# Where sixteen steps of weight sums stand in a fused encoder block, which queue carries them, and which engine does some small evacuations

## The chip, the cores and the metric

One core of one Trainium2 chip runs the whole program; its engines are TensorE (PE: matmuls, and PEld its weight loads), VectorE (DVE), ScalarE (ACT), GpSimd (POOL) and SyncE (SP, which here only issues DMAs). The metric is the device time of one execution in microseconds (us), lower is better; a kernel's time is the median of its runs.

## The reference

One layer of a streaming encoder on x of 256 tokens by 1024, in float32. Each stage adds its normalised result to x:

```python
x += 0.5 * rms_post(swiglu(rms_pre(x)))            # ffn 1, width 2816
h  = rms_pre(x); q_a, f_a, i_a, g_a, q_b, k_b, v_b, f_b, gates = split(h @ w_in)
f  = lb + (1 - lb) * sigmoid(f_a); k = 1 - f; q = silu(q_a)
o_t = S_t^T q_t,  S_t = diag(f_t) S_{t-1} + k_t i_t^T       # recurrence, 8 heads of 128
A  = rms(o) * silu(g_a)
B  = softmax(q_b k_b^T / sqrt(128) + decay of f_b, causal) v_b   # "FoX"
y  = sigmoid(gate_A) * (A @ w_branch_a) + sigmoid(gate_B) * (B @ w_branch_b)
x += rms_post(y @ w_out)
x += rms_post(cross_attention(rms_pre(x), rms(mem)))  # the memory stage, 4 heads
x += 0.5 * rms_post(swiglu(rms_pre(x)))            # ffn 2
```

## The kernel before

The kernel is one program for one core, written for a scheduler that keeps each engine's order close to the order of the text; `issue_after(x)` puts an instruction behind x in that order, and `after(i)` does so for the i-th matmul of a log, with priority. Nothing loops at run time.

**Weights.** Every weight passes through TensorE as two float32r parts. `load_split` (L129) loads 512 KB, [128, 1024], by SP's queue into one of 4 `raw` buffers; ScalarE casts it to `hi` (L137) and VectorE takes the rest, `lo = raw - hi` (L138), each into one of 8 buffers. A projection does three matmuls per block: hi by hi, hi by lo, lo by hi (`proj_tok` L177, `proj_col` L186); four units of weights make a chunk of 512 columns. An instruction on SP's queue that waits holds all that stand behind it.

**Order of the stages.** ffn 1; then the mixer's projections i_a, f_a, q_a (L779 to L836), the recurrence with gf (g_a and f_b's eight columns together, in three chunks of 344), k_b and q_b (L935 to L996), FoX's scores, v_b and the gates (L1032 to L1127), the branches and w_out, the memory stage (mk, mq, mv, the attention, mo, L1205 to L1305), ffn 2.

**The recurrence** is done by levels, m = 0, 1, 2, ..., 32, 64, 128, for two groups of four heads: `products(m)` multiplies k and q tiles on TensorE, `grow(m)` multiplies halves of q and k by the decay products on VectorE (L898, L903, L904, and the next products at L908), `keep` stores the products. The products of one level need the growth of the level before. They are put among the projection matmuls of gf, k_b and q_b by counts in the log, `R_AT` (L45); the scheduler places the growth and the splits of the weights on VectorE in between.

**The sums.** ffn 2 multiplies by a Strassen-like scheme in four "quads", and this needs sums of its weights. They are made early, in 16 steps, `steps` (L745): `load_step` (L749) brings 2 x 512 KB into one of two `wide` slots, `at` (L762) makes four VectorE adds of 128x512 on it (L771 to L774) and stores 2 x 512 KB to DRAM (L776), then calls for the next load. `SUMS_AT` (L56) names the places where the steps stand: `(name, c)` is the c-th evacuation of that projection. Only the first two loads go by SP's queue; the other loads and all stores by GpSimd's queue. Loads after the fourth wait for the gates' bias rows, which use a `wide` buffer (L1112).

**Evacuations.** f is scaled and shifted by VectorE (L821, eight of 128x256) and k = 1 - f too (L823). q is silu(z): ScalarE's Sigmoid (L834), then VectorE's product (L835). g_a likewise: Sigmoid (L946), then one VectorE instruction that scales and multiplies (L947, six of them). FoX's softmax is scaled by VectorE (L1057).

**The tail.** `post_last` (L346) ends the second token half: the squares' sums on ScalarE, a square root there (L357), two small Newton steps on VectorE (L364 to L368), then the last scaling of 1024 columns: 256 by ScalarE and GpSimd (L373, L374), 512 and 256 by VectorE (L376), three stores by two queues. `act_evac` (L409) issues a small Sqrt to a scratch tile (L417) after a Silu of the last quad, so that ScalarE's table is loaded.

Of the kernel before, what the change touches and what calls it, by code (L numbers as in the profile page):

```python
# [16 lines left out]
P = 128  # L17
D = 1024
T = 256
# [59 lines left out]
def block_kernel(ctx: ExitStack, tc: tile.TileContext, wts, head_in, gf_in, x_in, mem_in, memT_in, cols, rows, fbias, masks, out):  # L79
# [42 lines left out]

    cache = {}
    loads = []

    def parts_of():
        return [wp.tile([P, D], F32R, tag=t, name=nm(t), bufs=8) for t in ("hi", "lo")]

    def load_split(src, n=512):  # L129

        raw = wp.tile([P, D], F32, tag="raw", name=nm("raw"), bufs=4)
        hi, lo = parts_of()
        r, h, l = raw, hi, lo
        if n < 512:
            r, h, l = (p.rearrange("p (k n) -> p k n", k=2)[:, :, :n] for p in (raw, hi, lo))
        loads.append(nc.sync.dma_start(r, src).ins)
        S.copy(h, r)  # L137
        V.tensor_tensor(out=l, in0=r, in1=h.bitcast(F32), op=ALU.subtract)  # L138
        return hi, lo

    def unit(name, i):
# [204 lines left out]
    def post_last(ps, h, grow, factor):  # L346

        s = s1(2, name="ss2")
        ts = []
        for j in range(2):  # L350
            ssq(s[:, j : j + 1], ps[j])
            if j == 0:
                sums = s1(name="v")
                V.tensor_scalar(out=sums, in0=s[:, 0:1], scalar1=D * EPS, scalar2=None, op0=ALU.add)
            else:
                y = s1(name="y")
                S.activation(y, s[:, 1:2], AF.Sqrt, bias=sums)  # L357
                v = s1(name="v")
                V.tensor_tensor(out=v, in0=s[:, 1:2], in1=sums, op=ALU.add)
            t = sp.tile([P, 512], F32, tag="z2", name=nm("post"), bufs=3)  # L360
            V.scalar_tensor_tensor(out=t, in0=ps[j], scalar=-factor * 16.0, in1=grow[:, j * 512 : (j + 1) * 512], op0=ALU.mult, op1=ALU.mult)
            ts.append(t)
        z = s1(name="y")
        V.reciprocal(z, y)  # L364
        t = s1(name="t")
        V.scalar_tensor_tensor(out=t, in0=v, scalar=z, in1=z, op0=ALU.mult, op1=ALU.mult)
        r = s1(name="y")
        V.scalar_tensor_tensor(out=r, in0=t, scalar=3.0, in1=z, op0=ALU.subtract, op1=ALU.mult)  # L368
        for eng, a, b, queue in ((G, 512, 768, nc.scalar), (V, 0, 512, nc.sync), (V, 768, 1024, nc.sync)):
            xh = xs[:, h, a:b]  # L370
            t = ts[a // 512][:, a % 512 : a % 512 + b - a]
            if eng is G:
                S.activation(t, t, AF.Copy, scale=r)  # L373
                G.tensor_tensor(out=xh, in0=t, in1=xh, op=ALU.add)  # L374
            else:
                V.scalar_tensor_tensor(out=xh, in0=t, scalar=r, in1=xh, op0=ALU.mult, op1=ALU.add)  # L376
            queue.dma_start(out[h * P : (h + 1) * P, a:b], xh)


    def ffn(w_in, w_dn, X, r2, n_tok, i_row, quads, sums, first_half, second_half=None):  # L380
# [366 lines left out]
    brows = []  # L747

    def load_step():  # L749
        if len(slots) < len(steps) and (brows or len(slots) < TO_GATES):  # L750
            c, q, i = steps[len(slots)]
            W = wp.tile([P, 2, 2, 512], F32, tag="wide", name=nm("wide"), bufs=2)
            for e in range(2):
                part, src = W[:, e].rearrange("p j n -> p (j n)"), wts[_AT["f2_in"] + 4 * (c + e - 1) + 2 * q + i]
                if len(slots) < 2:
                    with tc.issue_after(loads[-1]):
                        nc.sync.dma_start(part, src)
                else:
                    G.dma_start(part, src)
            slots.append(W)  # L760

    def at(name, c=0):  # L762

        if (name, c) not in SUMS_AT:
            return
        k = SUMS_AT.index((name, c))
        (u, q, i), W = steps[k], slots[k]
        last = next(x for x in reversed(nc.cur_bb.bb.instructions) if x.engine == mybir.EngineType.DVE)
        t1, t4, t3, t2 = (W[:, a, b] for a in range(2) for b in range(2))
        with tc.issue_after(last):  # L770
            V.tensor_tensor(out=t1, in0=t1, in1=t3, op=ALU.add)  # L771
            V.tensor_tensor(out=t3, in0=t3, in1=t2, op=ALU.add)
            V.tensor_tensor(out=t2, in0=t1, in1=t2, op=ALU.add)  # L773
            V.tensor_tensor(out=t4, in0=t2, in1=t4, op=ALU.add)  # L774
        for e in range(2):
# [35 lines left out]
    for c in range(2):  # L811
        u = chunk("f_a", c)
        f, k = m4([P, 4, T], n="f"), m4([P, 4, T], n="k")
        for j in range(2):
# [8 lines left out]
        V.tensor_scalar(out=k, in0=f, scalar1=-1.0, scalar2=1.0, op0=ALU.mult, op1=ALU.add)  # L823
        fT.append(f)
        kT_.append(k)
    for c in range(2):
        u = chunk("q_a", c)
        q = m4([P, 4, T], n="q")
        for j in range(2):
            js = slice(2 * j, 2 * j + 2)  # L830
            ps = proj_col2(X2, u, (2 * j, 2 * j + 1))
            z = sp.tile([P, 2, T], F32, tag="z2", name=nm("z2"), bufs=3)
            V.tensor_tensor(out=z, in0=ps, in1=bc(row2, [P, 2, T], 1), op=ALU.mult)
            S.activation(q[:, js], z, AF.Sigmoid)  # L834
            V.tensor_tensor(out=q[:, js], in0=q[:, js], in1=z, op=ALU.mult)  # L835
        qT_.append(q)  # L836


# [100 lines left out]
    for c in range(3):  # L939
        u = [load_split(gf_in[4 * c + i], GF) for i in range(4)]  # L940
        n = min(GF, D - c * GF)
        for h in range(2):
            ps = mm()
            proj_tok(ps[:, :GF], X2, u, h, GF)
            sg = sp.tile([P, 512], F32, tag="z2", name=nm("z2"), bufs=3)[:, :n]
            sig_last = S.activation(sg, ps[:, :n], AF.Sigmoid, scale=r2[h]).ins  # L946
            V.scalar_tensor_tensor(out=Gt[h][:, c * GF : c * GF + n], in0=ps[:, :n], scalar=r2[h], in1=sg, op0=ALU.mult, op1=ALU.mult)  # L947
            if n < GF:
                V.tensor_scalar(out=zf[h], in0=ps[:, n:GF], scalar1=r2[h], scalar2=None, op0=ALU.mult)


    fz = sp.tile([8, T], F32, tag="fz", name="fz", bufs=1)
# [20 lines left out]
    for c in range(2):  # L973
        for name, lst, sc in (("k_b", kb_, 1.0), ("q_b", qb_, 1.0 / math.sqrt(128.0))):
# [3 lines left out]
            for j in range(2):  # L978
                ps = proj_col2(X2, u, (2 * j, 2 * j + 1))
                for i in range(2):  # L980
                    V.scalar_tensor_tensor(out=t[:, 2 * j + i], in0=ps[:, i], scalar=sc, in1=row2, op0=ALU.mult, op1=ALU.mult)
            lst.append(t)
            if c == 0 and name == "k_b":
                forget(m + 30)
# [47 lines left out]
    def fox_scores(g):  # L1032
        k, q = kb_[g], qb_[g]
        for h in range(2):
# [22 lines left out]
            V.tensor_tensor(out=p, in0=p, in1=bc(sm, [P, 4, ns], 2), op=ALU.mult)  # L1057
            ps_[g, h] = p

    def fox_pT(g):  # L1060
# [32 lines left out]
    for c in range(2):  # L1093
        u = chunk("v_b", c)
        t = m4([P, 2, 512], n="v_b")
        for h in range(2):
            ps = mm()
            proj_tok(ps, X2, u, h)
            S.activation(t[:, h, :], ps, AF.Copy, scale=r2[h])
        vb_.append(t)  # L1100
    for h in range(2):
        with after(len(log) - L_OA * (2 - h)):
# [5 lines left out]
    def gates(c):  # L1108
        u = chunk("gates", c)
        z = m4([P, 2, 512], n="zg")  # L1110
        if c == 0:
            brows.append(wp.tile([P, 4, 512], F32, tag="wide", name=nm("brow"), bufs=2))  # L1112
        brow = brows[0][:, c]
# [8 lines left out]

    m = len(log)
    gates(0)
    load_step()
    for g in range(2):
        with after(m + F_T[g]):  # L1127
            fox_pT(g)
# [3 lines left out]

    memT_s = [m4([P, 4, T], n="memT") for _ in range(2)]
    for j in range(2):
        nc.sync.dma_start(memT_s[j], memT_in[:, 4 * j : 4 * j + 4, :])
    M = Pair()
    for kb in range(KB):
        gain_split(M, kb, memT_s[kb // 4][:, kb % 4, :], G_KV)
    rm = []
    for h in range(2):  # L1140
        ms = m4([P, D], n="ms")
        nc.sync.dma_start(ms, mem_in[:, h])
# [6 lines left out]
    load_step()  # L1149
    g2 = load_row(1)  # L1150
    Y = Pair()

# [244 lines left out]
```

## Time and profile before

| | us |
|---|---|
| three runs, median (lowest to highest) | 785.71 (785.20 to 786.02) |
| the profiled execution | 785.17 |
| its span in the profile | 783.4 |
| TensorE busy | 774.3 |
| VectorE busy | 646.2 |
| ScalarE busy | 468.4 |

The profile is one execution; what lies around its span is 1.77 us. Instructions are named by engine, line of the kernel, operation and tiles (out<-in). In a listing the first column is the start in us from the span's start and the second the duration; brackets say how long the engine stood idle before and what released it. Instructions that follow one another on VectorE overlap a little in the records, so their cost is read from start to start.

### The profile page before, as it was taken

The page shows a single profiled execution, that of the slowest core. Times are in us where ns is not written, and L with a number is a line of the kernel's source. Part 1 is how long each engine was busy: PE and PEld are TensorE (multiplying, and loading weights), DVE is VectorE, ACT ScalarE, POOL GpSimd, SP SyncE. Part 2 cuts the span into 40 slices and gives each one's busy share as a digit, 9 for nine tenths or more (in the row PEclk, how much of TensorE's full clock was granted, in tenths as well). Part 3 has the DMA queues.
Part 4 walks back from the last instruction along what each step waited for, and adds up shares of the span by engine and source line. Part 5 has one row for each costly group of instructions (what it writes and reads, how often), then busy time and mean ns, then how long its engine had stood idle before and what let it go on. Part 6 is the DMA issues. An engine that isn't in the chain of part 4 may idle for free.

```text
span 783.4 us, 13175 instructions
## 1 busy us (share of the span) xinstructions
PE 774.3 (99%) x5004; PEld 669.9 (86%) x5004; DVE 646.2 (82%) x1004; ACT 468.4 (60%) x704; POOL 48.4 (6%) x81
## 2 busy tenths in 40 slices
PE   9999999999999999999999999999999999999996
PEld 7888888888899999998888888999888888888884
DVE  7889989968798898578777886998787889888864
ACT  7665664756752447347674444744646758677763
POOL 0000000000121100200001221011110000000000
PEclk9999999999999999999999999999999999999999
DMA  9794484476687655753479999579875279899831
GB/s 349 249 327 154 155 309 161 147 233 245 251 305 257 183 191 164 232 212 121 152 278 341 377 338 378 203 275 375 319 226 185 83 261 388 311 314 323 339 122 54
DMA packets 57392, 193.61 MB, mean 247 GB/s; under 512 B 6249, under 2 KB 9713, under 8 KB 57329
## 3 DMA queue, kind: packets, MB, share of 16 engines
q1 hardware_dynamic: 48080, 159.60, 57.9%
q0 software_dynamic: 9104, 33.04, 12.1%
q8 instruction: 39, 0.64, 0.3%
q14 instruction: 25, 0.20, 0.1%
q10 hardware_dynamic: 144, 0.13, 0.0%
HBM read 174.92 MB, written 17.83 MB: 246 GB/s over the span
## 4 chain that ended last, share of the span: by engine, by line
PE 99%; ACT 0%; DVE 0%; issue 0%; DVEq 0%; ACTq 0%
PE mm L93 64%; PE acc L93 28%; PE tr L93 4%; PE tr L395 1%; PE tr L315 1%; PE tr L1067 0%; PE tr L1158 0%; PE tr L1264 0%; ACT L357 0%; PE tr L406 0%; DVEq L1393 0%; DVE xs L376 0%; ACT hT L156 0%; ACT y L357 0%; ACT junk L243 0%
## 5 line engine op out<-in xcount | busy, mean ns | idle before, releaser
L138 DVE TENSOR_TENSOR lo<-raw,hi 128x1024 fp32r<-128x1024 f32 (+1 forms) x228 | 271.3, 1205 | 53.0 <-ACT hi L137 49.2
L137 ACT CAST hi<-raw 128x1024 fp32r<-128x1024 f32 (+1 forms) x228 | 232.1, 1036 | 118.2 <-PE mm L93 69.5
L93 PE MATMUL mm<-lo,hT 128*128 128x512 f32 (+1 forms) x448 | 171.2, 386 | 0.0
L93 PE MATMUL mm<-hi,hT 128*128 128x512 f32 (+1 forms) x448 | 170.7, 385 | 0.0
L93 PE MATMUL mm<-hi,lT 128*128 128x512 f32 (+1 forms) x448 | 170.4, 384 | 0.0
L93 PE MATMUL acc<-hi,act 128*128 128x512 f32 x352 | 113.2, 391 | 0.0
L93 PE MATMUL mm<-hT,hi 128*128 128x256 f32 x384 | 109.0, 284 | 0.1
L93 PE MATMUL mm<-hT,lo 128*128 128x256 f32 x384 | 109.0, 284 | 0.0
L93 PE MATMUL mm<-lT,hi 128*128 128x256 f32 x384 | 108.9, 284 | 0.0
L93 PEld LDWEIGHTS mm<-hi,hT 128*128 128x128 f32 x448 | 84.1, 188 | 16.1 <-ACT hT L271 0.7
L93 PEld LDWEIGHTS mm<-hi,lT 128*128 128x128 f32 x448 | 84.1, 188 | 15.8 <-DVE lT L272 0.5
L93 PEld LDWEIGHTS mm<-lo,hT 128*128 128x128 f32 x448 | 84.0, 188 | 15.0 <-DVE lo L138 0.4
L93 PEld LDWEIGHTS acc<-hi,act 128*128 128x128 f32 x352 | 65.9, 188 | 13.7 <-DVE act L157 0.2
L93 PEld LDWEIGHTS mm<-hT,hi 128*128 128x128 f32 x384 | 73.6, 192 | 0.5 <-issue 0.3
L93 PEld LDWEIGHTS mm<-lT,hi 128*128 128x128 f32 x384 | 73.6, 192 | 0.1
L93 PEld LDWEIGHTS mm<-hT,lo 128*128 128x128 f32 x384 | 73.6, 192 | 0.1
L93 PE MATMUL acc<-lo,act 128*128 128x512 f32 x176 | 69.0, 392 | 0.0
L157 DVE TENSOR_TENSOR lo<-wide,hi 128x1024 fp32r<-128x1024 f32 x40 | 47.9, 1219 | 1.5 <-ACT hi L156 1.1
L156 ACT CAST hi<-wide 128x1024 fp32r<-128x1024 f32 x40 | 41.5, 1052 | 11.5 <-DVE wide L494 7.5
L776 POOL DMA_DIRECT2D sums<-wide x32 | 23.6, 738 | 357.8 <-DVE wide L773 240.8
L93 PEld LDWEIGHTS acc<-lo,act 128*128 128x128 f32 x176 | 33.1, 188 | 6.7
L93 PE MATMUL mm<-hi,sh 128*128 128x512 f32 x96 | 37.5, 390 | 0.0
(243 smaller groups left out, 1126.8 us busy)
## 6 DMA issues: line engine op xcount, KB each, us to landing
raw<-in_wts_dram SPq DMA_DIRECT2D x232, 512.0 KB, 5.1
sums<-wide POOLq DMA_DIRECT2D x32, 512.0 KB, 6.2
wide<-sums SPq DMA_DIRECT2D x32, 512.0 KB, 6.9
wide<-in_wts_dram POOLq DMA_DIRECT2D x28, 512.0 KB, 6.7
wide<-in_wts_dram SPq DMA_DIRECT2D x12, 512.0 KB, 6.4
raw<-in_gf_dram SPq DMA_DIRECT2D x12, 344.0 KB, 4.9
head<-in_head_dram SPq DMA_DIRECT2D x8, 388.0 KB, 5.7
grow<-in_rows_dram SPq DMA_DIRECT2D x4, 512.0 KB, 8.9
```

The costliest lines, as they stand in the source:

```text
L93: log.append(PE.matmul(*args, **kw).ins)
L137: S.copy(h, r)
L138: V.tensor_tensor(out=l, in0=r, in1=h.bitcast(F32), op=ALU.subtract)
L156: S.copy(hi, src)
L157: V.tensor_tensor(out=lo, in0=src, in1=hi.bitcast(F32), op=ALU.subtract)
L315: PE.transpose(ps[:, j * P : (j + 1) * P], src(kb), ident)
L395: PE.transpose(trv[:, j, h * P : (h + 1) * P], ats[c, h][:, j * P : (j + 1) * P], ident)
L776: G.dma_start(sums[u][2 * e : 2 * e + 2, q, :, i * 512 : i * 512 + 512].rearrange("k p n -> p k n"), W[:, e])
```

## The change

- `SUMS_AT`: ten steps now stand among the projections from i_a to q_b (before, four), six behind the gates and in the branches as before, none in the memory stage.
- All loads and stores of the sums go by SP's queue. A store is called for when 8 more weight loads have been written (`TO_STORE`), the next load 4 weight loads after that (`TO_LOAD`); both are put behind the newest weight load. New are `later` and `tick`, which keep this list.
- ScalarE scales and shifts f, makes k, and scales FoX's softmax (four instructions where VectorE had one). q and g_a become ScalarE's Silu directly, without VectorE's product; the first Silu stands behind k.
- The gates' bias rows lie in `z2` tiles of 128x512 and come, like memory's inputs, by GpSimd's queue.
- `post_last` scales 2 x 512 columns on VectorE and stores by SP's queue; the warm-up Sqrt stands behind the last Silu of ffn 2.

Because the scheduler fits the rest around this, other instructions move as well. The matmuls are the same 5004. In the changed program 18 projection matmuls stand between the level-32 and the level-64 products, 46 before; and the split of the fourth unit of the first q_b chunk stands behind the growth of level 32 and one add, where it stood ahead of that growth.

```diff
-SUMS_AT = (
-    ("i_a", 1), ("f_a", 0), ("f_a", 2), ("f_a", 3), ("gates", 1), ("gates", 3), ("br_a", 0), ("br_b", 0),
-    ("br_a", 1), ("br_b", 1), ("mk", 1), ("mk", 3), ("mq", 0), ("mq", 1), ("mv", 1), ("ao", 0),
-)
-TO_GATES = 4
+SUMS_AT = (("i_a", 1), ("f_a", 1), ("f_a", 3), ("q_a",1), ("q_a",3), ("gf",1), ("gf",3), ("gf",5), ("k_b", 1), ("q_b", 1), ("gates", 1), ("gates", 3), ("br_a", 0), ("br_b", 0), ("br_a", 1), ("br_b", 1),)
+TO_STORE = 8
+TO_LOAD = 4
...
+    due = []
+
+    def later(n, f):
+        due.append((len(loads) + n, f))
+
+    def tick():
+        while due and due[0][0] <= len(loads):
+            due.pop(0)[1]()
...
         V.tensor_tensor(out=l, in0=r, in1=h.bitcast(F32), op=ALU.subtract)
+        tick()
         return hi, lo
...
-        for eng, a, b, queue in ((G, 512, 768, nc.scalar), (V, 0, 512, nc.sync), (V, 768, 1024, nc.sync)):
...
+        for j, (t, xh) in enumerate(zip(ts, x_halves(h))):
+            V.scalar_tensor_tensor(out=xh, in0=t, scalar=r, in1=xh, op0=ALU.mult, op1=ALU.add)
+            nc.sync.dma_start(out[h * P : (h + 1) * P, j * 512 : (j + 1) * 512], xh)
...
-            if c == NFF - 1 and (c, 1 - h) in ats and not first_half:
+            if len(ats) == 2 * NFF - 1 and not first_half:
...
-                if len(slots) < 2:
-                    with tc.issue_after(loads[-1]):
-                        nc.sync.dma_start(part, src)
-                else:
-                    G.dma_start(part, src)
...
+        for e in range(2):
+            with tc.issue_after(loads[-1]):
+                nc.sync.dma_start(W[:, e].rearrange("p j n -> p (j n)"), wts[_AT["f2_in"] + 4 * (c + e - 1) + 2 * q + i])
...
         k = SUMS_AT.index((name, c))
+        while len(slots) <= k:
+            due.pop(0)[1]()
...
-        for e in range(2):
-            G.dma_start(sums[u][2 * e : 2 * e + 2, q, :, i * 512 : i * 512 + 512].rearrange("k p n -> p k n"), W[:, e])
-        load_step()
+
+        def store():
+            for e in range(2):
+                with tc.issue_after(loads[-1]):
+                    nc.sync.dma_start(sums[u][2 * e : 2 * e + 2, q, :, i * 512 : i * 512 + 512].rearrange("k p n -> p k n"), W[:, e])
+            later(TO_LOAD, load_step)
+
+        later(TO_STORE, store)
...
-                V.tensor_scalar(out=f[:, i], in0=f[:, i], scalar1=olb[:, hd : hd + 1], scalar2=lbv[:, hd : hd + 1], op0=ALU.mult, op1=ALU.add)
+                S.activation(f[:, i], f[:, i], AF.Identity, bias=lbv[:, hd : hd + 1], scale=olb[:, hd : hd + 1])
...
-            S.activation(q[:, js], z, AF.Sigmoid)
-            V.tensor_tensor(out=q[:, js], in0=q[:, js], in1=z, op=ALU.mult)
+            V.tensor_tensor(out=q[:, js], in0=ps, in1=bc(row2, [P, 2, T], 1), op=ALU.mult)
+            with tc.issue_after(k_last):
+                S.activation(q[:, js], q[:, js], AF.Silu)
+            at("q_a", 2 * c + j)
...
-            sig_last = S.activation(sg, ps[:, :n], AF.Sigmoid, scale=r2[h]).ins
-            V.scalar_tensor_tensor(out=Gt[h][:, c * GF : c * GF + n], in0=ps[:, :n], scalar=r2[h], in1=sg, op0=ALU.mult, op1=ALU.mult)
+            sig_last = S.activation(Gt[h][:, c * GF : c * GF + n], ps[:, :n], AF.Silu, scale=r2[h]).ins
...
-            V.tensor_tensor(out=p, in0=p, in1=bc(sm, [P, 4, ns], 2), op=ALU.mult)
+            for i in range(4):
+                S.activation(p[:, i], p[:, i], AF.Copy, scale=sm[:, i : i + 1])
...
-        with tc.issue_after(loads[-1]):
-            nc.sync.dma_start(brow, rows[4 + c // 2, c % 2 * 512 : c % 2 * 512 + 512].partition_broadcast(P))
+        brow = sp.tile([P, 512], F32, tag="z2", name=nm("brow"), bufs=3)
+        G.dma_start(brow, rows[4 + c // 2, c % 2 * 512 : c % 2 * 512 + 512].partition_broadcast(P))
```

More of the change, by code (lines that the diff above doesn't have):

```diff
@@ L368, in post_last @@
         V.scalar_tensor_tensor(out=r, in0=t, scalar=3.0, in1=z, op0=ALU.subtract, op1=ALU.mult)
-        for eng, a, b, queue in ((G, 512, 768, nc.scalar), (V, 0, 512, nc.sync), (V, 768, 1024, nc.sync)):
[L370 to L374, printed above, removed]
-            else:
-                V.scalar_tensor_tensor(out=xh, in0=t, scalar=r, in1=xh, op0=ALU.mult, op1=ALU.add)
-            queue.dma_start(out[h * P : (h + 1) * P, a:b], xh)
+        for j, (t, xh) in enumerate(zip(ts, x_halves(h))):
+            V.scalar_tensor_tensor(out=xh, in0=t, scalar=r, in1=xh, op0=ALU.mult, op1=ALU.add)
+            nc.sync.dma_start(out[h * P : (h + 1) * P, j * 512 : (j + 1) * 512], xh)
     def ffn(w_in, w_dn, X, r2, n_tok, i_row, quads, sums, first_half, second_half=None):
@@ L746, in block_kernel @@
     slots = []
-    brows = []
     def load_step():
-        if len(slots) < len(steps) and (brows or len(slots) < TO_GATES):
-            c, q, i = steps[len(slots)]
-            W = wp.tile([P, 2, 2, 512], F32, tag="wide", name=nm("wide"), bufs=2)
-            for e in range(2):
-                part, src = W[:, e].rearrange("p j n -> p (j n)"), wts[_AT["f2_in"] + 4 * (c + e - 1) + 2 * q + i]
-                if len(slots) < 2:
-                    with tc.issue_after(loads[-1]):
-                        nc.sync.dma_start(part, src)
-                else:
-                    G.dma_start(part, src)
-            slots.append(W)
+        if len(slots) == len(steps):
+            return
+        c, q, i = steps[len(slots)]
+        W = wp.tile([P, 2, 2, 512], F32, tag="wide", name=nm("wide"), bufs=2)
+        for e in range(2):
+            with tc.issue_after(loads[-1]):
+                nc.sync.dma_start(W[:, e].rearrange("p j n -> p (j n)"), wts[_AT["f2_in"] + 4 * (c + e - 1) + 2 * q + i])
+        slots.append(W)
     def at(name, c=0):
@@ L774, in at @@
             V.tensor_tensor(out=t4, in0=t2, in1=t4, op=ALU.add)
-        for e in range(2):
-            G.dma_start(sums[u][2 * e : 2 * e + 2, q, :, i * 512 : i * 512 + 512].rearrange("k p n -> p k n"), W[:, e])
-        load_step()
+        def store():
[4 more added lines that the diff above has]
+        later(TO_STORE, store)
     iv = [m4([P, 2, 512], n="iv") for _ in range(2)]
@@ L820, in block_kernel @@
                 hd = 4 * c + i
-                V.tensor_scalar(out=f[:, i], in0=f[:, i], scalar1=olb[:, hd : hd + 1], scalar2=lbv[:, hd : hd + 1], op0=ALU.mult, op1=ALU.add)
+                S.activation(f[:, i], f[:, i], AF.Identity, bias=lbv[:, hd : hd + 1], scale=olb[:, hd : hd + 1])
             at("f_a", 2 * c + j)
-        V.tensor_scalar(out=k, in0=f, scalar1=-1.0, scalar2=1.0, op0=ALU.mult, op1=ALU.add)
+        k_last = S.activation(k, f, AF.Copy, bias=1.0, scale=-1.0).ins
         fT.append(f)
@@ L831, in block_kernel @@
             ps = proj_col2(X2, u, (2 * j, 2 * j + 1))
-            z = sp.tile([P, 2, T], F32, tag="z2", name=nm("z2"), bufs=3)
-            V.tensor_tensor(out=z, in0=ps, in1=bc(row2, [P, 2, T], 1), op=ALU.mult)
-            S.activation(q[:, js], z, AF.Sigmoid)
-            V.tensor_tensor(out=q[:, js], in0=q[:, js], in1=z, op=ALU.mult)
+            V.tensor_tensor(out=q[:, js], in0=ps, in1=bc(row2, [P, 2, T], 1), op=ALU.mult)
+            with tc.issue_after(k_last):
+                S.activation(q[:, js], q[:, js], AF.Silu)
+            at("q_a", 2 * c + j)
         qT_.append(q)
@@ L944, in block_kernel @@
             proj_tok(ps[:, :GF], X2, u, h, GF)
-            sg = sp.tile([P, 512], F32, tag="z2", name=nm("z2"), bufs=3)[:, :n]
-            sig_last = S.activation(sg, ps[:, :n], AF.Sigmoid, scale=r2[h]).ins
-            V.scalar_tensor_tensor(out=Gt[h][:, c * GF : c * GF + n], in0=ps[:, :n], scalar=r2[h], in1=sg, op0=ALU.mult, op1=ALU.mult)
+            sig_last = S.activation(Gt[h][:, c * GF : c * GF + n], ps[:, :n], AF.Silu, scale=r2[h]).ins
             if n < GF:
                 V.tensor_scalar(out=zf[h], in0=ps[:, n:GF], scalar1=r2[h], scalar2=None, op0=ALU.mult)
+            at("gf", 2 * c + h)
     fz = sp.tile([8, T], F32, tag="fz", name="fz", bufs=1)
@@ L981, in block_kernel @@
                     V.scalar_tensor_tensor(out=t[:, 2 * j + i], in0=ps[:, i], scalar=sc, in1=row2, op0=ALU.mult, op1=ALU.mult)
+                at(name, 2 * c + j)
             lst.append(t)
@@ L1099, in block_kernel @@
             S.activation(t[:, h, :], ps, AF.Copy, scale=r2[h])
+            at("v_b", 2 * c + h)
         vb_.append(t)
@@ L1110, in gates @@
         z = m4([P, 2, 512], n="zg")
-        if c == 0:
-            brows.append(wp.tile([P, 4, 512], F32, tag="wide", name=nm("brow"), bufs=2))
-        brow = brows[0][:, c]
-        with tc.issue_after(loads[-1]):
-            nc.sync.dma_start(brow, rows[4 + c // 2, c % 2 * 512 : c % 2 * 512 + 512].partition_broadcast(P))
+        brow = sp.tile([P, 512], F32, tag="z2", name=nm("brow"), bufs=3)
+        G.dma_start(brow, rows[4 + c // 2, c % 2 * 512 : c % 2 * 512 + 512].partition_broadcast(P))
         for h in range(2):
@@ L1134, in block_kernel @@
     for j in range(2):
-        nc.sync.dma_start(memT_s[j], memT_in[:, 4 * j : 4 * j + 4, :])
+        G.dma_start(memT_s[j], memT_in[:, 4 * j : 4 * j + 4, :])
     M = Pair()
@@ L1141, in block_kernel @@
         ms = m4([P, D], n="ms")
-        nc.sync.dma_start(ms, mem_in[:, h])
+        G.dma_start(ms, mem_in[:, h])
         rm.append(rstd_x([ms[:, 0:512], ms[:, 512:]]))
```

2 lines of the change are left out of this document (removed).

## The prediction

> **What bounds the kernel now.** I read the page's busy times and the chain of work that ended last first, then the waits of TensorE.
>
> ```profile
> span 783.4 us, 13175 instructions
> PE 774.3 (99%) x5004; PEld 669.9 (86%) x5004; DVE 646.2 (82%) x1004; ACT 468.4 (60%) x704; POOL 48.4 (6%) x81
> PE 99%; ACT 0%; DVE 0%; issue 0%; DVEq 0%; ACTq 0%
> ```
>
> ```profile
> PE tr L93 <- DVE ones L206: 1.1, 1, 1.1
> ```
>
> The chain is TensorE from end to end, and its list of waits has one row: 1.1 us, once, at the start. So no work taken off another engine and no transfer made cheaper can shorten the middle. The change can gain only behind the last matmul, and it loses wherever TensorE is now made to wait. The question is how much room the engines beside it have. Busy time by stage answers that (us, then PE, PEld, DVE, ACT and POOL busy, TensorE's clock, DMA share, GB/s):
>
> ```profile
> 205.00:256.30 51.30, 51.30 (x412) 50.51 (x411) 41.34 (x61) 25.71 (x33) 7.19 (x12) 1.00 0.83 294
> 256.30:306.40 50.10, 50.05 (x1119) 48.15 (x1119) 45.03 (x81) 27.19 (x40) 3.74 (x8) 1.00 0.59 181
> 480.00:620.00 140.00, 139.88 (x868) 125.19 (x868) 116.12 (x221) 82.69 (x150) 14.40 (x23) 1.00 0.72 256
> ```
>
> The second row is the stretch in which the recurrence's level products stand between the gf, k_b and q_b projections: VectorE is busy 45.0 of 50.1 us, so it has 5.1 us of room. The third row is the memory stage: TensorE is short of 0.12 us in 140. What is freed there can be worth next to nothing; I put it at 0, at most 0.5 us over the whole run.
>
> **The change, part by part.**
>
> *The tail.* These rows are the end of the run (start, duration; the matmul is the last one), with the stores' landing times from the page's list of DMA issues.
>
> ```profile
> 775.29 0.39 PE L93 MATMUL acc<-hi,act 128*128 128x512 f32 x1
> ...
> 776.27 0.19 ACT L243 ACTIVATION_READ_ACCUMULATOR junk<-acc 128x1 f32 x1
> 776.49 1.28 ACT L357 ACT_TABLE_LOAD   x1
> 776.50 0.69 DVE L361 SCALAR_TENSOR_TENSOR post<-acc,grow 128x512 f32<-128x512 f32 x1 [1.24 <-ACT junk L243]
> 777.11 0.15 DVE L359 TENSOR_TENSOR v<-ss,v 128x1 f32<-128x1 f32 x1
> 777.78 0.29 ACT L357 ACTIVATE y<-ss,v 128x1 f32<-128x1 f32 x1
> 778.11 0.17 DVE L364 RECIPROCAL y<-y 128x1 f32<-128x1 f32 x1 [0.85 <-ACT y L357]
> ...
> 778.76 1.61 DVE L376 SCALAR_TENSOR_TENSOR xs<-post,y,xs 128x512 f32<-128x512 f32 x2
> ...
> 779.54 1.19 SPq L377 DMA_DIRECT2D out_dram<-xs  x2
> ```
>
> ```profile
> out_dram<-xs SPq DMA_DIRECT2D x3, 256.0 KB, 2.0
> ...
> out_dram<-xs SPq DMA_DIRECT2D x1, 128.0 KB, 1.9
> ```
>
> The square root at 777.78 stands behind a table load of 1.28 us, and VectorE waits 0.85 us for it. The load is there because the warm-up of Sqrt is issued behind a Silu that is not the last one, and Silu's table came back. The change issues it behind the really last Silu, well ahead of the tail. Then the root runs at 776.49 and ends before 776.8; next late is VectorE itself, which is through its product and sum at 777.11 + 0.15 = 777.26. The reciprocal starts at about 777.28 in place of 778.11: 0.83 us sooner. Behind it the old tail has two VectorE passes (1.61 us, a 512-wide one and, as the code has it, a 256-wide one, the listing grouping them) and GpSimd's quarter; the new one has two 512-wide passes of 0.60 start to start. From 778.76 − 0.83 = 777.93 these end at 777.93 + 0.60 + 0.69 = 779.2 in place of 780.37, and the last transfer, now 256 KB, takes 2.0 in place of 1.9. Bounds 0.7 (a semaphore's hop more) to 1.1; I take **−0.9 us**.
>
> *VectorE's work in the stretch 256.3 to 306.4.* The levels form a chain: products on TensorE, growth of q and k on VectorE, next products. Durations come from these two views, a listing of VectorE just ahead of the level-64 products, and the stretch's groups (busy, mean ns):
>
> ```profile
> 302.87 1.23 DVE L138 TENSOR_TENSOR lo<-raw,hi 128x1024 fp32r<-128x1024 f32 x1 [1.89 <-ACT hi L137]
> 304.01 0.68 DVE L903 TENSOR_TENSOR q<-q,aux 128x512 f32<-128x512 f32 x1
> 304.61 0.68 DVE L904 TENSOR_TENSOR k<-k,aux 128x512 f32<-128x512 f32 x1
> 305.21 0.68 DVE L903 TENSOR_TENSOR q<-q,aux 128x512 f32<-128x512 f32 x1
> 305.82 0.68 DVE L904 TENSOR_TENSOR k<-k,aux 128x512 f32<-128x512 f32 x1
> ```
>
> ```profile
> L138 DVE TENSOR_TENSOR lo<-raw,hi 128x688 fp32r<-128x688 f32 x7 | 6.1, 872 | 0.2
> ...
> L898 DVE TENSOR_TENSOR q<-q,f 128x1024 f32<-128x1024 f32 x2 | 2.4, 1221 | 0.7 <-PE acc L93 0.7
> L947 DVE SCALAR_TENSOR_TENSOR G<-mm,rstd,z 128x344 f32<-128x344 f32 x4 | 2.3, 565 | 0.6 <-ACT z L946 0.6
> ...
> L835 DVE TENSOR_TENSOR q<-q,z 128x512 f32<-128x512 f32 x1 | 0.7, 691 | 0.0
> ```
>
> ```profile
> L773 DVE TENSOR_TENSOR wide<-wide 128x512 f32<-128x512 f32 x16 | 11.0, 688 | 0.3
> ```
>
> Start to start, a 512-wide add costs 0.60, a 1024-wide split or product 1.14, a 688-wide split 0.79 us; rows overlap by some 0.08. From the last q evacuation (TensorE sets its time, 256.31) to the end of the level-32 growth, the changed program's order on VectorE differs so: six products into G leave for ScalarE's Silu (6 × 0.49 = −2.9); one q product leaves (−0.6); three 1024-wide splits, ten before and seven now, stand behind the growth (−3.4); eighteen adds of sums come in (those of q_a 3, gf 1, gf 3, gf 5 and the first two of k_b 1; 18 × 0.60 = +10.8). Before, that work took 45.1 us and ended at 306.5. Now it is 45.1 − 2.9 − 0.6 − 3.4 + 10.8 = 49.0 us, and would end at 305.3 if VectorE never idled.
>
> *When TensorE wants it.* The products stand elsewhere too:
>
> ```profile
> 301.24 1.21 PE L93 MATMUL acc<-q,k 128*32 128x32 f32 x64
> 302.37 0.39 PE L93 MATMUL mm<-lT,hi 128*128 128x256 f32 x1
> 302.59 0.28 PE L93 MATMUL mm<-hT,lo 128*128 128x256 f32 x1
> 302.71 0.28 PE L93 MATMUL mm<-hT,hi 128*128 128x256 f32 x1
> 302.83 0.29 PE L93 MATMUL mm<-lT,hi 128*128 128x256 f32 x1
> ...
> 308.08 1.09 PE L93 MATMUL acc<-q,k 128*64 128x64 f32 x30
> ```
>
> Between the level-32 and the level-64 products stand 46 projection matmuls of 0.12 us; in the changed order 18. So TensorE comes to the level-64 products not at 308.08 but at about 302.37 + 18 × 0.12 + 0.15 = 304.7, and to the second recurrence's half of them 0.55 us later, 305.25. The old growth ended 1.6 us ahead of 308.08; the new one, at best 305.3, has no room. Behind these products TensorE has 5 more matmuls (0.6 us), then wants the split of the fourth q_b unit, which VectorE does after the growth and one more add: 0.60 + 1.14 = 1.74 against 0.55 + 0.6 = 1.15, so another 0.6 us. Without any idle time on VectorE the stall is 0.05 + 0.6 = 0.65 us; each us of idle adds one.
>
> *The transfers.* Stores and loads of sums move from GpSimd's queue to SP's, where the weights are issued in order. Landing times (min, median, max) at two places of the trace, first of three weight loads behind four wide halves on SP, then of four weight loads while the same kind of stores went out by GpSimd:
>
> ```profile
> 184.31 1.94 SPq L757 DMA_DIRECT2D wide<-in_wts_dram  x4
> 186.35 2.28 SPq L136 DMA_DIRECT2D raw<-in_wts_dram  x3
> ```
>
> ```profile
> DMA to landing us min/median/max: 8.7/9.0/9.3
> ```
>
> ```profile
> DMA to landing us min/median/max: 4.6/5.3/5.5
> ```
>
> ```profile
> wide<-in_wts_dram SPq DMA_DIRECT2D x12, 512.0 KB, 6.4
> ```
>
> A store on SP waits for VectorE's fourth add, a load for the landing of the store before it in its slot, and all weight loads behind stand still meanwhile. In the changed order gf 3's two wide halves stand between and behind gf 1's two stores, and behind them the third k_b unit's load. Ahead of the end of gf 1's adds VectorE has the evacuation, eight adds, four small splits, two 1024-wide products, four growths and some 1.3 us of masks: 0.6 + 4.8 + 3.2 + 2.3 + 2.4 + 1.3 = 14.6, so they end near 271; four issues of 0.43 each later the second load half is out, near 272.8, and it lands 6.4 later, at 279.2. VectorE has two small and two large splits, four growths and 0.8 of masks before gf 3's first add (1.6 + 2.3 + 2.4 + 0.8 = 7.1) and reaches it at 278.0: 1.2 us idle. The k_b load is issued near 272, behind four halves, lands after 8.7, and ScalarE's cast takes 1 us more: 281.9 against 280.7, another 1.2. That is 2.4 us; with 5.3 us for either landing both are in time and it is 0; with 9.3 for both it is about 4. I take 2.4, from the row of the same queue and position. The growth then ends at 305.3 + 2.4 = 307.7 and TensorE's stall is 2.45 + 0.6 = **+3.0 us** (0.65 to 4.8).
>
> A rule speaks against this. The Trainium skill, page "DMA: Bandwidth & Descriptors", section "Issuing engines are not separate DMA queues", says that transfers started by different engines run on the same 16 DMA engines and that only issue time depends on who starts them. By it the landing would be GpSimd's and the stall 0.65; the two landing rows here differ, but so does what else is in flight at the two places, so they do not refute it.
>
> *The other stages.* ScalarE takes 8 scalings of f, two of 1−f, and 16 scalings in FoX's softmax; it was busy 25.7 of 51.3 and about half elsewhere, and TensorE waited for none of it. VectorE loses these:
>
> ```profile
> L1057 DVE TENSOR_TENSOR p<-p,sm 128x512 f32<-128x512 f32 (+1 forms) x4 | 3.8, 949 | 0.0
> ```
>
> The scalings, four in a row per tile where VectorE made one pass of 0.95, stand ahead of the transposes, which stand some matmuls later in the new order. I take 0; bounds −0.5 and, about one such pass too late, +1. Fewer sums in the memory stage (6 × 2.4 us of VectorE): 0. The gate rows on GpSimd's queue: 0, since the weights that follow land sooner without them.
>
> **The sum**, against the profiled execution's 785.17 (span 783.4 and 1.77 around it): 785.17 − 0.9 + 3.0 = 787.3. The median of the three runs, 785.71, lies 0.54 above it: **787.8**.
>
> **The rivals.** *The queue does not matter (the other side).* If SP's in-order issue delays nothing that lands, VectorE idles only as TensorE lets it, the level-64 stall is 0.65 us or less, and the tail decides: 785.71 − 0.9 + 0.65 = 785.5, with up to 0.65 and 0.5 of the memory stage more in its favour, 784.3. For it: 5.3 us landings beside GpSimd's stores, a DMA share of 0.59 in the stretch. Against: the 8.7 to 9.3 row. It decides from landings of under some 6 us. Range 784.0 to 786.4. This is also the result by the skill's rule.
>
> *SP's queue closes in on itself.* Five steps end in the 50.1 us of the stretch, so those on one slot are 20 us apart; adds of 2.4, a store and a load of 9 each make 20.4, and some wait at the queue's head. If each of gf 3, gf 5, k_b 1 and q_b 1 comes 1.5 us late, idle is 6, the stall 6.05 + 0.6, and the time 785.71 − 0.9 + 6.65 = 791.5 (789.3 to 793). For it: every store now blocks weight loads. Against: the same trips took 5 to 7 us on GpSimd's queue.
>
> *FoX or the gates stall as well*: the forecast plus 1 us, 788.8.
>
> **How the numbers follow.** The forecast (its own range 786.4 to 789.2) 0.42; the queue does not matter 0.27; SP closes in 0.20; FoX as well 0.11. Below 784.7 and above 791.2 I leave some 0.2. About 0.2% or 1.57 us is what a measurement of this kernel tells from no change: slower starts at 787.28, faster at 784.14. The forecast's range lies two thirds beyond 787.28 (0.28), with 0.20 and 0.11: slower 0.59. Same: 0.14 of the forecast and 0.21 of the second case, 0.35. Faster: its lowest end, 0.06.
>
> **What would show it.** Right: the table load gone from the tail and the reciprocal near 0.8 us sooner after the last matmul; a TensorE wait of 2 to 3 us at the level-64 products for VectorE's q or k, then a smaller one for a lo; VectorE idle ahead of gf 3's first add, released by a DMA; the memory stage the same length with less VectorE and DMA. Wrong: no TensorE wait between 256 and 312 (second case), waits at several levels or weight loads landing after 10 us (third), waits after 345 (fourth).

## The result and the profile after

| | us |
|---|---|
| before, median of 6 runs in this comparison | 785.19 |
| changed, median of 6 runs (lowest to highest) | 794.23 (790.42 to 799.28) |
| ratio, 95% interval | 1.0116 (1.0093 to 1.0139) |
| the profiled execution of the changed kernel, its span | 796.39, 794.6 |

The change makes the kernel 9.0 us slower, where 2.1 was forecast and 791.2 was the upper end of the range. It also makes the time unsteady: six runs spread over 9 us, those of the kernel before over 1.1.

The page's first line and its chain, then TensorE's waits (engine, line and tile <- who released it: us in total, times, longest):

```profile
span 794.6 us, 13118 instructions
...
PE 75%; DVE 10%; DMA 9%; issue 3%; ACT 2%; SPq 1%; DVEq 0%; ACTq 0%
```

```profile
PE mm L91 <- DVE zf L951: 2.6, 1, 2.6
PE tr L91 <- DVE ct L1032: 2.0, 1, 2.0
PE acc L91 <- ACT q L838: 1.2, 1, 1.2
PE tr L322 <- DVE lT L279: 1.1, 1, 1.1
PE tr L91 <- DVE ones L213: 1.1, 1, 1.1
PE acc L91 <- ACT hT L278: 0.6, 1, 0.6
```

The chain, which was TensorE alone, now runs through VectorE, ScalarE and the transfers. No line of the list is the wait that was forecast, at the level-64 products for q or k. The stages, in the columns of the table shown before:

```profile
205.00:256.30 51.30, 51.30 (x408) 50.36 (x407) 35.78 (x48) 32.77 (x42) 0.00 (x0) 1.00 0.88 293
256.30:306.40 50.10, 46.24 (x1021) 44.29 (x1020) 45.00 (x82) 22.41 (x31) 2.27 (x6) 0.97 0.97 334
306.40:345.00 38.60, 38.60 (x399) 38.16 (x398) 28.85 (x42) 17.59 (x26) 5.88 (x7) 1.00 0.92 337
480.00:620.00 140.00, 138.76 (x859) 124.39 (x858) 101.42 (x184) 80.15 (x138) 0.00 (x0) 1.00 0.57 187
```

VectorE's load in the second row is what it was, 45.0 us. What changed is the last two columns: the DMA share there rose from 0.59 to 0.97 and what was moved from 181 to 334 GB/s. In the memory stage both fell, and TensorE gained nothing there, as forecast; it lost 1.1 us, the wait for `lT` (L279) in the list. How a late transfer reaches TensorE is read from the chain in order of time (start, duration):

```profile
275.28 7.81 DMA raw<-in_wts_dram
...
283.17 1.05 ACT hi L143
...
284.25 1.23 DVE lo L144
285.47 0.60 DVE wide L772
286.07 0.60 DVE q L907
...
289.15 0.60 DVE wide L773
289.75 0.15 DVE zf L951
289.90 0.04 issue
289.94 3.42 PE mm L91 x17
```

A weight load takes 7.8 us to land. ScalarE's cast waits for it, VectorE's split waits for the cast, and behind the split, in VectorE's order, stand an add, the growth of q and k, the last add and the small evacuation `zf` (L951), which alone keeps a PSUM buffer from TensorE. TensorE stands still for 2.6 us. And then it is slow:

```profile
286.00:289.90 3.90, 1.30 (x9) 1.01 (x7) 3.90 (x12) 1.52 (x2) 0.00 (x0) 1.00 1.00 344
289.90:293.30 3.40, 3.36 (x19) 3.14 (x19) 3.05 (x4) 2.06 (x3) 0.00 (x0) 0.61 0.93 324
...
353.90:358.70 4.80, 4.65 (x17) 3.82 (x18) 4.73 (x21) 0.96 (x4) 0.00 (x0) 0.67 0.56 218
```

The granted clock is 0.61 in the 3.4 us behind the stall and 0.67 in the 4.8 us behind the next (2.0 us, in FoX): 3.4 × 0.39 + 4.8 × 0.33 = 2.9 us more. With the five new waits, 2.6 + 2.0 + 1.2 + 1.1 + 0.6 = 7.5, this is 10.4 of the 12.0 us by which the last matmul came later in this execution (787.28 against 775.29).

### The profile page after: what moved, and what is told of

It is laid out like the page before. It is cut to its first block, busy times and chain, and to the rows that moved or that the text cites. A ratio compares the mean times of both kernels' runs of the same rounds, so it can differ in the third digit from the quotient of the medians.

```text
span 794.6 us, 13118 instructions
## 1 busy us (share of the span) xinstructions
PE 778.6 (98%) x5004; PEld 672.9 (85%) x5004; DVE 632.0 (80%) x980; ACT 478.9 (60%) x728; POOL 13.2 (2%) x28
## 4 chain that ended last, share of the span: by engine, by line
PE 75%; DVE 10%; DMA 9%; issue 3%; ACT 2%; SPq 1%; DVEq 0%; ACTq 0%
PE mm L91 47%; PE acc L91 23%; DMA raw<-in_wts_dram 7%; DVE lo L144 3%; PE tr L91 3%; ACT hi L143 1%; PE tr L396 1%; DMA raw<-in_gf_dram 1%; DVE k L908 1%; DMA sums<-wide 1%; PE tr L322 1%; DVE q L907 1%; DMA head<-in_head_dram 1%; DVE wide L773 1%; DVE wide L771 1%
## 5 line engine op out<-in xcount | busy, mean ns | idle before, releaser
L91 PE MATMUL mm<-hi,sl 128*128 128x512 f32 x96 | 37.4, 390 | 0.0
```

What stands on the lines that cost most here:

```text
L91: log.append(PE.matmul(*args, **kw).ins)
```

## The experiments

Two theories stood at first. H: a store or load that waits at the head of SP's queue holds the weights behind it. V, the forecast's own: ten steps are too much work for VectorE in this stretch. A third, D, came from the windows above: the transfers' bytes are too many there. The results (medians in us; each ratio against runs of the kernel before on the same chip, with its 95% interval):

| run | median | ratio |
|---|---|---|
| e1_new_places_gpsimd | 801.44 | 1.0218 (1.0190 to 1.0246) |
| e2_old_places_sp | 789.31 | 1.0050 (1.0031 to 1.0069) |
| e3_old_places_gpsimd | 785.68 | 1.0006 (0.9996 to 1.0015) |
| e4_before_new_tail | 784.38 | 0.9987 (0.9977 to 0.9996) |
| f1_no_adds | 794.86 | 1.0124 (1.0108 to 1.0139) |
| f2_no_transfers | 784.92 | 0.9998 (0.9989 to 1.0007) |
| f4_seven | 791.32 | 1.0077 (1.0053 to 1.0100) |
| g1_softmax_on_vector | 786.29 | 1.0013 (1.0003 to 1.0023) |
| h1_half_bytes | 788.56 | 1.0031 (1.0017 to 1.0046) |
| h2_no_waits | 796.00 | 1.0128 (1.0109 to 1.0148) |
| i1_gpsimd_no_adds | 806.39 | 1.0264 (1.0248 to 1.0280) |
| i2_before_scalar_moves | 785.75 | 1.0004 (0.9995 to 1.0013) |
| j0_data19 | 797.82 | 1.0152 (1.0133 to 1.0172) |
| j1_raw6 | 800.75 | 1.0191 (1.0172 to 1.0209) |

**Places and queue, one at a time (e1, e2, e3).**

```diff
 e1, e3: load_step and store
-            with tc.issue_after(loads[-1]):
-                nc.sync.dma_start(...)
+            G.dma_start(...)
 e2, e3: SUMS_AT as before
```

> The changed kernel, with loads and stores of the sums issued by GpSimd's queue; the ten places among the recurrence's projections stay. Theory H (a store or load that waits at the head of SP's queue holds the weights behind it): the stalls near 261, 290 and 352 us go, the time falls from about 794 to 785 to 787. Theory V (ten steps are too much work for VectorE there, whatever the queue): 790 or more, with TensorE still waiting for VectorE near 290 and 352.

> The changed kernel with the old sixteen places of the sums; their transfers stay on SP's queue. H: still slow, 788 to 793, with VectorE idle for weights' splits because weight loads are issued late. V: the recurrence is relieved, 784.5 to 786.

> Both undone: old places and GpSimd's queue; left of the change are the work moved to ScalarE, the gates' rows and memory's inputs on GpSimd's queue, and the tail. If these cost nothing: 785.2 - 0.9 = 784.3. If ScalarE's Silu or the softmax scalings delay TensorE: 786 or more, with a wait for ScalarE in TensorE's list.

H fell at once as the whole story: with the new places GpSimd's queue is not a cure but worse, 801.4. With the old places the same swap of queue does what H says, 789.3 on SP and 785.7 on GpSimd. On SP's queue the new places cost 4.9 us (794.2 less 789.3), on GpSimd's 15.8, and the better queue depends on them. What e2 loses it loses elsewhere than the changed kernel: TensorE is busy 49.78 of 50.10 us in the stretch of the recurrence, and 137.28 of 140.00 in the memory stage (139.88 in e3).

**The adds or the transfers (f1, f2).**

```diff
 f1: at
-        with tc.issue_after(last):
-            V.tensor_tensor(...)   # all four
 f2: load_step, from the third step on; store; sum_of
+        if len(slots) >= 2:
+            slots.append(slots[-2])
+            return
-            for e in range(2): ... nc.sync.dma_start(sums[u]...)
-   loads.append(nc.sync.dma_start(W[:, q], sums[c][(0, 3, 2, 1)[k], q]).ins)
+   loads.append(nc.sync.dma_start(W[:, q], wts[_AT[w_in] + 4 * c - 4 + (2 * k + q) % 4]).ins)
```

> The changed kernel with the four adds of each of the sixteen steps left out: loads and stores go on as before, of unsummed weights, so the output is not the reference's. Theory V (VectorE's work bounds the stretch 256 to 306): the stalls go, some 785 to 786. Theory D (the transfers bound it: the DMA share there rose from 0.58 to 0.97): VectorE has 24 us less to do and the time stays at 789 or more, with ScalarE waiting for weights. Neither excludes the other: a fall to between says both.

> The changed kernel with all adds but without the transfers of the sums after the first two steps' loads: the adds work on the same two slots over and over, nothing is stored, and the last stage reads plain weights in place of sums (as many bytes), so the output is not the reference's. D: the stalls go, 785 to 786, although VectorE has all its work. V: 789 or more.

This pair decides between V and D. Without the adds nothing is won (794.9); without the transfers all is (784.9). One thing more differs from the changed kernel: in f1, f2, f4, h1 and h2 the scheduler put 46 projection matmuls between the level-32 and the level-64 products, as in the kernel before, where the changed kernel has 18. These runs can be compared with each other, and they do not try the stall that was forecast at the level-64 products. The stages of f2:

```profile
205.00:256.30 51.30, 51.30 (x407) 50.28 (x406) 38.13 (x53) 33.38 (x44) 0.00 (x0) 1.00 0.57 179
256.30:306.40 50.10, 50.10 (x1124) 48.57 (x1124) 50.02 (x90) 27.97 (x42) 2.94 (x7) 1.00 0.51 168
306.40:345.00 38.60, 38.60 (x350) 38.26 (x348) 28.41 (x44) 17.05 (x26) 4.69 (x6) 1.00 0.67 235
```

VectorE is busy 50.02 of 50.10 us, with no room at all, and TensorE 50.10 of 50.10. The level-32 growth ends at 305.8 us, where 305.3 was forecast without idle time. So the forecast's count of VectorE's work was about right, and a full VectorE that is fed in time delays nothing in this order. With 18 matmuls TensorE would have wanted the last of this growth at 303.16 + 18 × 0.12 + 0.15 + 0.55 = 306.0 by the forecast's own sum, an estimate that leaves it in time as well. The second row also gives an account that the prediction lacked. Without sums 168 GB/s are moved. A step loads and stores 4 × 512 KB, 2.1 MB; five steps in 50.1 us are 209 GB/s more, 377 in all. The changed kernel moved 334 there with a share of 0.97. What is short, 43 GB/s over 50 us, is 2.2 MB or 6.4 us at that rate, by this estimate most of the loss of 9.0. That 334 is the most that can be moved is not shown: between 318 and 338 us the same kernel moved 376 GB/s while TensorE was busy throughout, and run i1 below moved 394 over 51.3 us.

**Bytes or waits in the queue (h1, h2).** Both leave the adds out as f1 does.

```diff
 h1: half of each transfer
-  nc.sync.dma_start(W[:, e]..., wts[...])
+  nc.sync.dma_start(W[:, e, 0], wts[...][:, :512])
-  nc.sync.dma_start(sums[u][2 * e : 2 * e + 2, ...], W[:, e])
+  nc.sync.dma_start(sums[u][2 * e, ...], W[:, e, 0])
 h2: the stores' source
-  nc.sync.dma_start(sums[u][...], W[:, e])
+  nc.sync.dma_start(sums[u][...], xs[:, e].rearrange("p (k n) -> p k n", k=2))
```

> As the run without adds, but each load and store of the sums moves half its columns: same queue, same order, same waits, half the bytes (the last stage reads plain weights in place of sums; the output is not the reference's). If bytes bound it (theory D): 786 to 788. If what counts is that a store or load waiting at the head of SP's queue holds the weights (theory H): the waits shrink only as far as the transfers get shorter, 789 to 793.

> As the run without adds, with all bytes, but the stores read a tile that nothing writes at the time, so that no store waits for a load and no load for a store: same queue, same number and size of transfers, no wait at the queue's head but for the weights' own buffers (the stored values are not sums; the output is not the reference's). H: 785 to 787. D: 792 or more, with a DMA share of 0.9 and more from 256 to 345 us.

All bytes without the sums' waits at the queue's head: 796.0, as slow as ever. Half the bytes with the waits: 788.6, two thirds of the loss gone, though between the two ranges that were expected (786 to 788 and 789 to 793). With the new places H is out as the main cause, by h2. The same windows for h2, the second and third stage:

```profile
256.30:306.40 50.10, 43.49 (x987) 41.61 (x986) 31.97 (x56) 19.34 (x25) 2.27 (x6) 0.93 0.84 301
306.40:345.00 38.60, 38.60 (x399) 38.23 (x399) 28.59 (x43) 19.66 (x31) 5.34 (x7) 1.00 0.91 328
```

VectorE has nearly a third less to do than in the changed kernel, and TensorE loses 6.6 us of 50.1. The share is 0.84 while this happens, where 0.9 and more was expected, so the share alone would not have told it.

TensorE does not lose these 6.6 us as in the chain shown above. Its waits of over 1.1 us in h2, and the row of h2's page for a DMA queue that the profile calls "instruction":

```profile
PE mm L91 <- issue: 4.1, 1, 4.1
PE acc L91 <- issue: 2.5, 1, 2.5
```

```profile
q8 instruction: 39, 0.64, 0.3%
```

"issue" means that the profile shows nothing that TensorE waited for: no late cast, split or evacuation. f1 has the same two waits (3.7 and 2.2 us). But the trace's DMA records have loads of 16 KB on the instruction queue, seven of them in this stretch of h2. Two landed at 268.86 and 296.04 us, and the two waits ended at 270.26 and 297.46, 1.4 us behind each. All 17 such waits of TensorE in ten of the runs end 1.2 to 1.6 us behind such a landing. It looks as if TensorE then waits for its own instructions, whose loads come late beside the sums' transfers; no run tried this by itself.

**Rate or landing time (j0, j1).** Weight loads have four `raw` buffers, so a longer landing could hold back their issue even where the rate suffices.

```diff
 j1 (and the data pool of j0):
-  raw = wp.tile([P, D], F32, tag="raw", name=nm("raw"), bufs=4)
+  raw = wp.tile([P, D], F32, tag="raw", name=nm("raw"), bufs=6)
-  mp = ctx.enter_context(tc.tile_pool(name="data", bufs=21))
+  mp = ctx.enter_context(tc.tile_pool(name="data", bufs=19))
```

> Control for the next run: the changed kernel with 19 buffers of the data pool in place of 21, nothing else. It should stay at 794 (790 to 799); if it is slower, the next run is to be read against this one.

> The changed kernel with 6 raw buffers for weight loads in place of 4 (and 19 data buffers, to make room). If landing time against four loads in flight is what lets weights come late (latency theory): loads are issued some 10 us earlier, the time falls to 785 to 789. If the rate of the transfers itself is short (bandwidth theory, shares of 0.9 and more): earlier issue only lengthens the landing, 791 or more.

The control came out slower than the changed kernel, its median of 797.8 within the latter's spread. More buffers do not help: 800.8. The weights were late less often: ScalarE's casts stood idle for loads in `raw` for 7.8 us from 256.3 to 345 us, 35.8 in the control. So these waits alone do not set the time. The weights' landing from 256.3 to 345 us (min, median, max), in the changed kernel and then with six buffers:

```profile
DMA to landing us min/median/max: 5.2/6.4/9.5
```

```profile
DMA to landing us min/median/max: 3.3/8.0/12.7
```

Earlier issue made the median landing longer, 8.0 in place of 6.4 (6.4 in the control too), as a short rate would have it. The Trainium skill, page "DMA: Bandwidth & Descriptors", section "Where 436 GB/s comes from", gives some 358 GB/s as the memory's limit for one core and says that it binds transfers like these; the 377 asked for here lie above it. The trace does not agree that this is a limit here, with the 376 and 394 GB/s named above.

**Fewer steps (f4), and the queue again (i1).**

```diff
 f4: SUMS_AT
-  ("q_a",3), ("gf",3), ("k_b",1)
+  ("mk",1), ("mk",3), ("mq",0)
 i1: e1 without the four adds
```

> The changed kernel with seven steps in place of ten among the recurrence's projections (q_a 3, gf 3 and k_b 1 are emptied, and mk 1, mk 3 and mq 0 are used again), SP's queue as changed. D and V both expect less than 794: by D the share of 0.97 falls to some 0.8 and the time to 787 to 790, what is left being stalls where SP's queue holds weights behind a store, one of them in the memory stage. If the queue alone counts: 789, as with the old places.

> The new places with the transfers on GpSimd's queue (801 us), the adds left out, so that VectorE waits for no load of a slot (unsummed weights are stored; the output is not the reference's). If the extra 7 us over SP's queue come from VectorE waiting for the slots' loads, whose round trips are as long as the steps' spacing: 794 or less, as with the adds left out on SP's queue. If they come from weights that land later beside a queue of their own: 800 again.

Seven steps in place of ten: 791.3, a third of the loss back, less than hoped for. And i1 refutes its first branch: without adds, so that VectorE waits for no slot's load, GpSimd's queue is slower still, 806.4. Its first two stages:

```profile
205.00:256.30 51.30, 51.30 (x372) 48.66 (x371) 30.38 (x51) 37.31 (x54) 14.14 (x23) 1.00 1.02 394
256.30:306.40 50.10, 41.13 (x735) 39.58 (x734) 28.12 (x45) 16.40 (x23) 13.05 (x24) 0.90 0.89 312
```

Freed of the adds, the sums' transfers run ahead and fill the DMA engines in the first stage (1.02, 394 GB/s); TensorE loses 9 us in the next. It had lost 8 already between 150 and 205 us (46.75 of 55.00 busy, at a share of 0.99). That SP's queue is the better one for the new places because it holds the sums' transfers back between the weights fits this, but was argued, not tried by itself.

**The small edits (e4, i2, g1).**

```diff
 e4: the old kernel with the new post_last and
-            if c == NFF - 1 and (c, 1 - h) in ats and not first_half:
+            if len(ats) == 2 * NFF - 1 and not first_half:
 i2: e4 with f, k, q's and g_a's Silu and the softmax's scaling on ScalarE
 g1: e3 with the softmax's scaling back
-            for i in range(4):
-                S.activation(p[:, i], p[:, i], AF.Copy, scale=sm[:, i : i + 1])
+            V.tensor_tensor(out=p, in0=p, in1=bc(sm, [P, 4, ns], 2), op=ALU.mult)
```

> The kernel before with the tail and the warm-up's place alone changed. By the prediction's term: 0.9 us faster (0.7 to 1.1), 784.3 beside 785.2, no table load behind the last matmul. If the table load was hidden: 785.2.

> The old kernel with the new tail and the work moved to ScalarE (f, k, Silu for q and g_a, the softmax's scaling); places, queues and gates as before. The third run, which has the other small edits besides, was 1.3 us above the old kernel with the new tail. If ScalarE's part makes this difference: 785.2 to 785.9; if the gates' rows, memory's inputs or the delayed transfers do: 784.4.

> Old places and GpSimd's queue as in the third run, with the softmax's scaling back on VectorE. That run was 1.3 us above the old kernel with the new tail. If ScalarE's scalings delay FoX's transposes, this one is 0.6 to 1.3 us faster, 784.4 to 785.1; if not, 785.7 again.

The tail is worth what was forecast: 784.38 beside 785.16 in the same comparison, 0.8 us. The moves to ScalarE seem to give it back: 785.75 beside 785.37, a ratio 0.0017 or 1.3 us above e4's, with intervals that just meet. Which of the moves it would be stays open. g1 does not tell: its times fall into two groups, five from 784.6 to 785.7 us and six from 786.3 to 787.9, and the profiled one, 787.6, has a wait of 1.8 us on "issue" that ends at 290.7 us, ahead of FoX's softmax. It ends 1.5 us behind an instruction load's landing, at a DMA share of 0.51 in the stretch, so such waits come without full transfers too. e4 is the fastest version of this study that computes the layer, 0.8 us below the kernel before.

## Why the prediction was wrong

The sign was right and the size was not, and the step that failed is "the transfers". The prediction followed them along one path, VectorE late with the level-32 growth, and put them at 2.4 us of idle time there. What the runs showed in its place: the transfers carry the whole loss (784.9 without them, 794.9 with them and without the adds), and they stop TensorE at other places. Their landing was not underrated: 8.7 us was taken, and from 256.3 to 345 us the weights landed after 6.4 in the median and 9.5 at most. But in that time ScalarE stood idle ahead of its casts, until such loads had landed, for 41.0 us in 22 waits, where it was 0.6 in 2 before (us, times; the changed kernel, then the kernel before):

```profile
  DMA raw<-in_wts_dram: 32.3, 15
...
  DMA raw<-in_gf_dram: 8.7, 7
```

```profile
  DMA raw<-in_wts_dram: 0.6, 2
```

Nor did the prediction add up bytes against the rate, although the stretch's row, 181 GB/s at a share of 0.59, was quoted: 209 on top of it makes 390. It asked how long one transfer takes, not whether all of them fit.

- *VectorE's work*, the other term: the growth's end was counted well (305.8 in f2, 305.3 forecast), and the work cost nothing by itself (f2 784.9; f1, without the adds, 794.9). The 3.0 us at the level-64 products did not appear in the changed kernel, which has the 18 matmuls ahead of them. Its growth ended late, at 311.1 us, but TensorE, held up before, came to these products at 311.1 too.
- *Where the stalls are*: at the first level's products (ScalarE's Silu of q behind a cast that waits for a load), at `zf`, and at FoX's first transposes behind late splits. In-order engines carry one late weight to whatever stands behind its cast and split. In f1 and h2 the two longest are the waits on "issue".
- *The third case*, SP closing in on itself, came nearest in time (791.5, against 794.2) for a mechanism that only holds in part: h2 takes those waits away and stays slow. The second case, in which the queue does not matter, fell both ways: SP costs 3.6 us with the old places (e2 less e3) and saves 7.2 with the new ones (e1 less the changed kernel; 11.5 without the adds, i1 less f1). With it fell the time of 785.5 that the prediction drew from the rule of the Trainium skill, page "DMA: Bandwidth & Descriptors", section "Issuing engines are not separate DMA queues", that only issue time depends on the engine that starts a transfer.
- *The tail*: −0.9 forecast, −0.8 measured; in the profile the last rows moved as worked out:

```profile
787.28 0.39 PE L91 MATMUL acc<-hi,act 128*128 128x512 f32 x1
...
788.48 0.29 ACT L364 ACTIVATE y<-ss,v 128x1 f32<-128x1 f32 x1
...
789.16 0.16 DVE L371 RECIPROCAL y<-y 128x1 f32<-128x1 f32 x1
...
790.58 0.99 SPq L378 DMA_DIRECT2D out_dram<-xs  x2
```

The reciprocal starts 1.88 us after the last matmul's start; it was 2.82.
- *ScalarE's new work* was put at 0 and costs some 1.3 us if i2 less e4 is taken as it stands. *The memory stage* was put at 0: its freed 6 steps and its share of 0.57 gave nothing, though the profiled execution has a wait of 1.1 us there.

Left open: whether the transfers cost this by their rate as a whole or by single loads that come late; half the bytes (share 0.71 and 236 GB/s in that stage) and seven steps still cost 2.9 and 6.1 us, where the rate on average suffices. Open too are how much of it goes through late weights and how much through late instruction loads, and which move to ScalarE costs.

## What to carry to other kernels

Where a change moves transfers into a stage, add up the stage's bytes first: what it moves now, plus what comes in, against the rates that the same trace shows for long. A sum near them is a warning and not a verdict: e3's first stage carried 340 GB/s at a share of 0.96 and TensorE lost nothing there, and h1 lost 2.9 us with 236 in the recurrence's stretch. Free time on a compute engine says nothing about this; the two runs that told it were one with the work and no transfers, and one with the transfers and no work. And where every engine waits in order, a late load reaches whatever stands behind it.

## What the runs showed of the hardware

Behind two stalls of TensorE in the changed kernel, of 2.6 and 2.0 us, the granted clock was 0.61 for 3.4 us and 0.67 for 4.8 us, which is 1.3 and 1.6 us more, half to four fifths of the stall again. It is not so behind every stall: the clock stayed at 1.00 for 3.0 us behind one of 2.5 us in f4 and for 3.4 us behind one of 2.6 us in e1. The Trainium skill, page "TensorE: Matmul & The Clock Gate", section "What's actually happening", has the clock fall after an idle window of about 3.4 us; here shorter stalls sufficed, but not always.

The queue from which the same transfers are issued moved the time by 3.6 us one way and 7.2 the other. And a wait of TensorE on "issue" ended, 17 times out of 17, 1.2 to 1.6 us behind the landing of a 16 KB load on the instruction queue.
